# Expert 0's rows picked by fp32 one-hot matmuls from SBUF instead of a gather, and three overflow branches nested in one

## The chip, the cores and the metric

The kernel runs on one core of a Trainium2 chip. The metric is the device time of one execution in microseconds. Three runs of the kernel before took 800.53, 800.73 and 804.94 us, a median of 800.73 us.

## What is computed

One encoder layer on 512 tokens of width 1024 in fp32: a mixer (grouped attention and a spatial gating unit), a cross-attention on 256 memory rows, and a hierarchical mixture of experts, with a last norm. Only the mixture is touched here. `h` below is `rms_norm(x, g_moe)`.

```python
def hierarchical_moe(h, w_rg, b_rg, w_re, b_re, w_gate, w_up, w_down):
    t = h.reshape(B * S, D)
    glog = (t @ w_rg + b_rg).astype(jnp.float32)
    gprob = jax.nn.softmax(glog, axis=-1)
    gval, gidx = lax.top_k(gprob, 1)                       # one of 4 groups
    elog = (t @ w_re + b_re).astype(jnp.float32).reshape(-1, N_GROUPS, EXPERTS_PER_GROUP)
    elog_sel = jnp.take_along_axis(elog, gidx[:, :, None], axis=1)[:, 0]
    evals, eidx = lax.top_k(elog_sel, TOP_K)               # two of its 4 experts
    ew = jax.nn.softmax(evals, axis=-1) * gval
    ...
    for e in range(N_EXPERTS):                             # 16
        he = jax.nn.silu(t @ w_gate[e]) * (t @ w_up[e])
        y = y + combine[:, e:e + 1] * (he @ w_down[e])
```

Each token goes to 2 of 16 experts, so an expert has 64 tokens on average. The kernel gives each expert a block of 128 places.

## The kernel before

**Layout and precision.** The tokens stand in 4 tiles of 128 (`NT`), the width in 8 slices of 128 (`KT`). An fp32 product is made of three fp32r matmuls (`mm3`, L214): high times high, low times high, high times low, where `split` (L210) makes the high part on ScalarE and the low part, the difference, on VectorE. Programs follow the order in which they are written, engine by engine, except that the instructions behind the overflow block form a second sequence.

**Weights.** `Weights` (L68) streams chunks of 1 MB, 128 x 2048, in one fixed order through SP's queue (`issue`, L91) into slots that hold raw chunks, 14 in the expert stage. `pump` (L101) converts half a chunk: ScalarE copies the high part (L113), VectorE subtracts to get the low part (L114; for one half per expert GpSimd does). `hold_low` puts the low parts off until `flush_low`. A finished half gives back its place for converted weights (`done`, L145), of which there are 6, and the next half is converted. `W.limit` bounds how far ahead chunks are fetched. Every expert has chunks 0 and 1 (gate), 2 and 3 (up), 4 and 5 (down).

**Routing.** `wco(t)` (L961) makes the last product of the cross-attention for token tile t, adds it to `xr`, and calls what the caller hangs in between. `rtrans` transposes the tile, `rlog` multiplies it with the router's weights (L996, L997), `rms_scale` (L268) squares the row on ScalarE and makes the norm's scale on VectorE, `h3out` (L984) writes the normed rows to `h3d` in HBM. `route` finds the two experts of each token (L1018 to L1027, 22 small VectorE instructions for two tiles), `route_hi` marks which is the higher, `pos` counts each token's place in its expert's block with triangular matmuls (L1045, L1048).

**From routing to experts.** For expert e, `oh_e` builds a one-hot matrix of tokens against places on VectorE (L1099), `ids_e` multiplies it with the token numbers on TensorE (L1106) and VectorE writes the result as integers (L1107), `gather` fetches the rows from `h3d` with an indirect DMA on GpSimd's queue (L1111), and `xtr` transposes them on TensorE (L276) and splits them. For expert 0 all of that stands ahead of the overflow block; `ids_e` of experts 1 to 4 (`AHEAD` = 5) stands behind it, and only then `xtr` of expert 0 (L1266).

**Overflow.** If an expert has more than 128 tokens, `overflow` (L1167) takes the others in blocks in a loop. Every engine reads the largest count from SBUF and tests it at L1174, three times in a row. No count is that large with these inputs, and nothing of the blocks is in the trace.

**An expert.** `expert_period(e)` (L1320) runs eight halves of gate and up (`gate_up`), in each 6 matmuls of 512 columns for two slices, with hooks after a half (j, i); `mid` is the Silu, `fin` multiplies gate with up on VectorE (L1286), `h_e` transposes the result (L276), `down_scatter` makes the down product and scatters the rows. `h_e` and `down_scatter` of e - 1 run inside the period of e.

## Time and profile before

| what | value |
|---|---|
| median of 3 runs | 800.73 us |
| the profiled execution, its own time | 801.3 us |
| its span, first to last instruction | 799.6 us |
| TensorE busy | 733.2 us, 92% |
| VectorE busy | 612.0 us, 77% |
| ScalarE busy | 463.3 us, 58% |
| GpSimd busy | 197.2 us, 25% |
| mean granted TensorE clock | 0.968 |
| bytes moved by DMA | 161.99 MB, 203 GB/s on average |

All times in rows are microseconds from the start of the span. TensorE's matmuls overlap, so the length of a group in a timeline includes the tail of its last matmul. A clock of 1.00 is 2.4 GHz, 0.50 is 1.2 GHz. The 1.7 us between span and execution lie outside the first and last instruction.

### The profile page before, as it was taken

How to read it: one execution, taken by the hardware profiler on the slowest of the kernel's cores; microseconds unless marked ns; L12 is line 12 of the kernel's file. 1: busy time of each engine (PE TensorE's matmuls, PEld its weight loads, DVE VectorE, ACT ScalarE, POOL GpSimd, SP SyncE). 2: the span in 40 equal slices, each digit the busy share in tenths (PEclk: the TensorE clock that was granted, in tenths of full speed). 3: DMA queues.
4: the chain of work that ended last, by engine and by line, in shares of the span. 5: the costliest groups of instructions: out<-in, count | busy, mean ns of one | idle time of the engine just before them, and what ended most of it. 6: DMA issues, size and time to landing. Idle time of an engine off the chain costs nothing. (4 is left out here: it accounts for less than half of the span.)

```text
span 799.6 us, 10588 instructions
## 1 busy us (share of the span) xinstructions
PE 733.2 (92%) x3839; PEld 610.4 (76%) x3840; DVE 612.0 (77%) x1029; ACT 463.3 (58%) x702; POOL 197.2 (25%) x136
## 2 busy tenths in 40 slices
PE   4887999999999999989999658999999999999891
PEld 4775899778788888889988546888878888888660
DVE  5869899988562434676775758998999999999766
ACT  4545676665433223343554327878878888887742
POOL 4425312231000010032221212333333322222332
PEclk9999999999999999998999869999999999999996
DMA  7303121111212245256237868999889999993082
GB/s 285 129 4 155 54 106 53 55 53 53 95 66 103 106 178 207 88 213 223 71 106 270 310 240 311 334 374 364 334 335 391 356 358 372 389 382 155 14 304 106
DMA packets 28430, 161.99 MB, mean 203 GB/s; under 512 B 5119, under 2 KB 5151, under 8 KB 12112
## 3 DMA queue, kind: packets, MB, share of 16 engines
q1 hardware_dynamic: 21392, 143.66, 47.8%
q0 software_dynamic: 6976, 17.54, 6.0%
q8 instruction: 33, 0.54, 0.3%
q14 instruction: 29, 0.24, 0.1%
HBM read 155.15 MB, written 14.16 MB: 212 GB/s over the span
## 5 line engine op out<-in xcount | busy, mean ns | idle before, releaser
L114 DVE TENSOR_TENSOR l_e<-r_e,h_e 128x1024 fp32r<-128x1024 f32 x178 | 227.7, 1324 | 24.1 <-ACT h_e L113 24.0
L113 ACT ACTIVATE h_e<-r_e 128x1024 fp32r<-128x1024 f32 x192 | 195.5, 1055 | 18.4 <-PE u_e L219 10.4
L1111 POOL DMA_INDIRECT xe<-h3d,ixall x16 | 24.6, 1538 | 137.5 <-PE pt_xt_e L276 94.6
L217 PE MATMUL g_e<-h_e,xh_e 128*128 128x512 f32 x128 | 52.3, 408 | 0.0
L217 PE MATMUL u_e<-h_e,xh_e 128*128 128x512 f32 x128 | 51.6, 403 | 0.0
L218 PE MATMUL g_e<-l_e,xh_e 128*128 128x512 f32 x128 | 50.9, 397 | 0.8 <-DVE l_e L114 0.8
L219 PE MATMUL g_e<-h_e,xl_e 128*128 128x512 f32 x128 | 50.8, 397 | 0.0
L218 PE MATMUL u_e<-l_e,xh_e 128*128 128x512 f32 x128 | 50.6, 395 | 0.0
L219 PE MATMUL u_e<-h_e,xl_e 128*128 128x512 f32 x128 | 50.6, 395 | 0.0
L217 PE MATMUL y_e<-h_e,hh_e 128*128 128x512 f32 x120 | 48.7, 406 | 1.7 <-ACT h_e L113 1.7
L218 PE MATMUL y_e<-l_e,hh_e 128*128 128x512 f32 x120 | 47.5, 396 | 0.8 <-DVE l_e L114 0.8
L114 POOL TENSOR_TENSOR l_e<-r_e,h_e 128x1024 fp32r<-128x1024 f32 x14 | 33.6, 2401 | 57.1 <-ACT h_e L113 57.1
L219 PE MATMUL y_e<-h_e,hl_e 128*128 128x512 f32 x120 | 47.4, 395 | 0.0
L560 ACT ACTIVATE p<-s,nm,qsc 128x512 f32<-128x512 f32 x32 | 25.0, 782 | 35.6 <-DVE nm L557 20.5
L1133 POOL DMA_INDIRECT ybuf<-y,ixall x15 | 31.2, 2083 | 26.0 <-ACT y L1309 23.9
L211 ACT ACTIVATE xh_e<-pt_xt_e 128x512 fp32r<-128x512 f32 x32 | 17.5, 595 | 30.6 <-PE pt_xt_e L276 30.5
L1309 ACT ACTIVATE y<-y_e 128x512 f32<-128x512 f32 x30 | 18.0, 599 | 23.6 <-PE y_e L219 23.6
L218 PEld LDWEIGHTS g_e<-l_e,xh_e 128*128 128x128 f32 x128 | 24.2, 189 | 6.2 <-DVE l_e L114 1.2
L219 PEld LDWEIGHTS g_e<-h_e,xl_e 128*128 128x128 f32 x128 | 24.2, 189 | 6.0 <-DVE xl_e L212 0.2
L219 PEld LDWEIGHTS u_e<-h_e,xl_e 128*128 128x128 f32 x128 | 24.1, 188 | 5.8
L217 PEld LDWEIGHTS g_e<-h_e,xh_e 128*128 128x128 f32 x128 | 24.3, 190 | 5.4 <-ACT xh_e L211 0.4
L218 PEld LDWEIGHTS u_e<-l_e,xh_e 128*128 128x128 f32 x128 | 24.1, 188 | 5.2
(431 smaller groups left out, 2144.3 us busy)
## 6 DMA issues: line engine op xcount, KB each, us to landing
r_e<-in_we_dram SPq DMA_DIRECT2D x95, 1024.0 KB, 8.0
r_a<-in_wf_dram SPq DMA_DIRECT2D x4, 1024.0 KB, 5.5
r_b<-in_wf_dram SPq DMA_DIRECT2D x4, 1024.0 KB, 4.8
r_y<-in_wf_dram SPq DMA_DIRECT2D x4, 1024.0 KB, 4.7
r_wo<-in_wf_dram SPq DMA_DIRECT2D x4, 1024.0 KB, 4.8
yt<-ybuf SPq DMA_DIRECT2D x4, 1024.0 KB, 11.1
xt<-in_x_dram SPq DMA_DIRECT2D x4, 512.0 KB, 5.7
r_q<-in_wf_dram SPq DMA_DIRECT2D x2, 1024.0 KB, 8.1
```

The lines of the kernel that those rows point to most:

```text
L113: A.activation(h, rr, AF.Copy)
L114: lo = lambda X=G if onpool >> i & 1 else V, l=l, rr=rr, h=h: X.tensor_tensor(l, rr, h, op=ALU.subtract)
L211: A.activation(dst_h, src, AF.Copy)
L217: T.matmul(ps, ah, bh, start=first and i == 0, stop=False)
L218: T.matmul(ps, ah, bl, start=False, stop=False)
L219: T.matmul(ps, al, bh, start=False, stop=last and i == n - 1)
L560: A.activation(pr, ps, AF.Exp, bias=nm, scale=qsc[t][:, h:h + 1], accum_out=sx)
L1111: G.indirect_dma_start(out=xe, out_offset=None, in_=h3d, in_offset=bass.IndirectOffsetOnAxis(ap=ix[:, 0:1], axis=0), bounds_check=S - 1, o ...
L1133: return G.indirect_dma_start(out=ybuf, out_offset=bass.IndirectOffsetOnAxis(ap=ix[:, 1:2], axis=0), in_=y, in_offset=None, bounds_check=2 ...
L1309: down(e, lambda n, ps: A.activation(y[:, n * 512:(n + 1) * 512], ps, AF.Copy), pumps)
```

## The change

The rows that `h3out` makes stay in SBUF: they are put into two borrowed raw slots (`borrow`), two token tiles each, until expert 0 has been picked, and still go to `h3d` for the other experts. Expert 0's transposed block is no longer gathered and transposed: `onehot_f32` builds an fp32 one-hot of two token tiles against expert 0's places, and `select(t, g)` multiplies four 128-wide slices of the rows with it into a PSUM bank (`xacc[g]`), summing over the four token tiles. Its two banks are split straight into `xT[0]`. `pos` and the one-hot of tiles 0 and 1 are hung into `wco(3)`; the transposes of tile 3 are copied by ScalarE instead of VectorE; `rlog(3)` uses a part of the bank of `pos`. `flush_low` moves behind the overflow block. Ahead of the experts only `ids_e` of 1 and 2 are left; those of 3 and 0 are hooks of expert 0's period, those of e + 4 of period e, and expert 1's `xtr` moves from hook (1, 1) to (2, 1). Chunks are fetched up to (0, 5) ahead of the experts instead of (2, 2). The two deeper overflow tests are nested in the first.

```diff
--- before.py
+++ after.py
@@ -31,7 +31,7 @@
 POOLJ = 1
 RSQ_MAGIC = float(0x5F3759DF - 2 ** 31)
 FILL_RATE = 1.4
-AHEAD = 5
+AHEAD = 4
 NR3 = 8
 NR4 = 2
 NTH = 6
@@ -82,6 +82,10 @@
         def spare(self, name, shape, dt=F32):
             pl, tag = self.raw_free.pop(0)
             return pl.tile(shape, dt, tag=tag, name=name)
+
+        def borrow(self, name, shape, dt=F32):
+            slot = self.raw_free.pop(0)
+            return slot[0].tile(shape, dt, tag=slot[1], name=name), slot
 
         def take(self, name, shape, dt=F32):
             pl, tag = self.raw_free.pop(0)
@@ -958,7 +962,7 @@
 
     h3T, h3r = {}, {}
 
-    def wco(t, between=None, after=None):
+    def wco(t, hooks):
         for n in range(2):
             w = W.chunk(cid[f"co{n}"])
             ps = bank("SO"[n], f"wc{t}_{n}")
@@ -967,22 +971,21 @@
             V.tensor_tensor(xs, ps, xs, op=ALU.add)
             if t == NT - 1:
                 W.done2(cid[f"co{n}"], 0)
-            if n == 0 and between:
-                between()
-        if after:
-            after()
+            for fn in hooks.get(n, ()):
+                fn()
         h3r[t] = rms_scale(xr[:, t, :], jkb, f"h3{t}")
 
     def rtrans(t):
         for g in range(0, KT, 4):
             pt = tr4(xr[:, t, :], g, f"h3{t}")
-            if t < NT - 1:
-                A.activation(h3T["t"][:, t % 2, g:g + 4], pt, AF.Copy)
-            else:
-                V.tensor_copy(h3T["t"][:, t % 2, g:g + 4], pt)
+            A.activation(h3T["t"][:, t % 2, g:g + 4], pt, AF.Copy)
+
+    h3s = {}
 
     def h3out(t):
-        jk = cr.tile([P, D], F32, tag="P2", bufs=2, name=f"h3{t}")
+        if t % 2 == 0:
+            h3s["t", t // 2], h3s["s", t // 2] = W.borrow(f"h3s{t // 2}", [P, 2, D])
+        jk = h3s[t] = h3s["t", t // 2][:, t % 2]
         if t < NT - 1:
             A.activation(jk, xr[:, t, :], AF.Copy, scale=h3r[t])
             G.tensor_tensor(jk, jk, gmoe, op=ALU.mult)
@@ -990,8 +993,8 @@
             V.scalar_tensor_tensor(jk, xr[:, t, :], h3r[t], gmoe, op0=ALU.mult, op1=ALU.mult)
         nc.sync.dma_start(h3d[t * P:(t + 1) * P, :], jk)
 
-    def rlog(t):
-        pl = bank("F", f"lg{t}")
+    def rlog(t, pl=None):
+        pl = bank("F", f"lg{t}") if pl is None else pl
         for k in range(KT):
             T.matmul(pl[:, :20], h3T["t"][:, t % 2, k], wrs[:, k], start=k == 0, stop=k == KT - 1)
         V.scalar_tensor_tensor(lgt[:, t, :], pl[:, :20], h3r[t], brs, op0=ALU.mult, op1=ALU.add)
@@ -1048,54 +1051,79 @@
         V.scalar_tensor_tensor(posm[:, c], pp[:, ts[0] * NE:(ts[-1] + 1) * NE].rearrange("p (t e) -> p t e", e=NE),
                                1.0, M[:, c], op0=ALU.add, op1=ALU.mult)
 
-    wco(0, lambda: (t2u(3, 0), t2u(3, 1)), lambda: pv2u(1))
+    wco(0, {0: [lambda: (t2u(3, 0), t2u(3, 1))], 1: [lambda: pv2u(1)]})
     cb_s.close()
     raw3 = ctx.enter_context(pool("raw3", side=L))
     W.add_raw(raw3, NR3, "ry")
     h3T["t"] = cr.tile([P, 2, KT, P], F32, tag="h3T", name="h3T")
+
     def upto(key):
         W.limit = cid[key] + 1
         W.issue()
 
-    def out_then(t, *keys):
-        h3out(t)
-        for k in keys:
-            upto(k)
-
-    upto((1, 3))
+    ohf = {}
+
+    def onehot_f32(e, i):
+        ohf[i] = ohp.tile([P, 2, P], F32, tag="oh", name=f"ohf{i}")
+        V.tensor_tensor(ohf[i], io128[:, None, :].to_broadcast([P, 2, P]),
+                        posm[:, 2 * i:2 * i + 2, e:e + 1].to_broadcast([P, 2, P]), op=ALU.is_equal)
+
+    xacc = {}
+
+    def select(t, g):
+        if t == 0:
+            xacc[g] = bank("F", f"xa{g}", (P, 4, P))
+        for k in range(4):
+            T.matmul(xacc[g][:, k, :], h3s[t][:, (4 * g + k) * P:(4 * g + k + 1) * P], ohf[t // 2][:, t % 2],
+                     start=t == 0 and k == 0, stop=t == NT - 1 and k == 3)
+
+    upto((0, 5))
     W.pump(2)
-    wco(1, lambda: (rtrans(0), out_then(0, (0, 5))))
+    wco(1, {0: [lambda: rtrans(0), lambda: h3out(0)]})
     rlog(0)
-    wco(2, lambda: (rtrans(1), out_then(1, (2, 0))))
+    wco(2, {0: [lambda: rtrans(1), lambda: h3out(1)]})
     rlog(1)
+    ohp = ctx.enter_context(pool("ohp", bufs=2, side=L))
     route((0, 1), V)
-    wco(3, lambda: (rtrans(2), out_then(2, (2, 1))), lambda: (rlog(2), rtrans(3)))
+    wco(3, {0: [lambda: rtrans(2), lambda: h3out(2), lambda: pos((0, 1)), lambda: onehot_f32(0, 0)],
+            1: [lambda: rlog(2), lambda: rtrans(3)]})
+    W.hold_low()
     route_hi((0, 1), V)
     V.tensor_tensor(Ms, M[:, 0], M[:, 1], op=ALU.add)
     cd_s.close()
     mx = ctx.enter_context(pool("moex", bufs=2, side=L))
     xes = [mx.tile([P, D], F32, bufs=1, name=f"xe{i}") for i in range(2)]
+    xslot = W.hl_free.pop(0)
+    rlog(3, pp[:, 64:84])
+    h3out(3)
+    W.pump(2)
+    G.memset(xes[1], 0.0)
     G.memset(xes[0], 0.0)
-    h3out(3)
-    G.memset(xes[1], 0.0)
-    xslot = W.hl_free.pop(0)
-    upto((2, 2))
-    W.hold_low()
-    W.pump(2)
-    rlog(3)
+    select(0, 0)
+    select(0, 1)
+    select(1, 0)
     route((2, 3), V)
-    route_hi((2, 3), V)
-    pos((0, 1))
     pos((2, 3))
     for t in (None, 2, 3):
         T.matmul(cnt[:, :NE], ones, M[:, t] if t else Ms, start=not t, stop=t == NT - 1)
+    select(1, 1)
+    onehot_f32(0, 1)
+    cmaxi = rt_([P, 1], "cmaxi", I32)
+    cmax = rt_([P, 1], "cmax")
+    cnts = rt_([P, NE], "cnts", I32)
+    V.tensor_reduce(cmax, cnt[:, :NE], axis=AX.X, op=ALU.max)
+    V.tensor_copy(cmaxi, cmax)
+    route_hi((2, 3), V)
+    for g in range(2):
+        for t in (2, 3):
+            select(t, g)
 
     cr_s.close()
     mo = ctx.enter_context(pool("moe", bufs=2, side=R))
     scat = []
 
     def onehot(name, pos):
-        oh = mx.tile([P, NT, P], F16, tag="oh", name=f"oh_{name}")
+        oh = ohp.tile([P, NT, P], F16, tag="oh", name=f"oh_{name}")
         V.tensor_tensor(oh, io128[:, None, :].to_broadcast([P, NT, P]), pos[:, :, None].to_broadcast([P, NT, P]),
                         op=ALU.is_equal)
         return oh
@@ -1144,17 +1172,8 @@
     def ids_e(e):
         ixs[e] = ids(f"e{e}", ohs[e], lambda t: vals[:, t, e, :], ixall[:, e])
 
-    oh_e(0)
-    cmaxi = rt_([P, 1], "cmaxi", I32)
-    cmax = rt_([P, 1], "cmax")
-    cnts = rt_([P, NE], "cnts", I32)
     posd = dr.tile([NE, P, NT], F32, name="posd")
     vald = dr.tile([NE, P, NT * 2], F16, name="vald")
-    V.tensor_reduce(cmax, cnt[:, :NE], axis=AX.X, op=ALU.max)
-    V.tensor_copy(cmaxi, cmax)
-    ids_e(0)
-    gather(ixs[0], xes[0])
-    W.flush_low()
 
     def overflow_tables(buf):
         pse = buf[:, :NE * NT].rearrange("p (e t) -> p e t", t=NT)
@@ -1170,15 +1189,15 @@
         xt = [mo.tile([P, KT, P], F32R, tag=n, bufs=1, name=f"ov{n}") for n in ("xh", "xl")]
         ht = [mo.tile([P, 4, P], F32R, tag=n, bufs=1, name=f"ov{n}") for n in ("hh", "hl")]
         nover = nc.values_load(cmaxi[0:1, 0:1], min_val=0, max_val=S)
-        for b in range(1, NT):
-            with tc.If(nover > b * P):
-                if b == 1:
-                    overflow_tables(oa)
-                    V.tensor_copy(cnts, cnt[:, :NE])
-                with tc.For_i(0, NE, 1) as ev:
-                    nev = nc.values_load(cnts[0:1, bass.ds(ev, 1)], min_val=0, max_val=S)
-                    with tc.If(nev > b * P):
-                        overflow_block(b, ev, oa, hl, xt, ht)
+        with tc.If(nover > P):
+            overflow_tables(oa)
+            V.tensor_copy(cnts, cnt[:, :NE])
+            for b in range(1, NT):
+                with tc.If(nover > b * P):
+                    with tc.For_i(0, NE, 1) as ev:
+                        nev = nc.values_load(cnts[0:1, bass.ds(ev, 1)], min_val=0, max_val=S)
+                        with tc.If(nev > b * P):
+                            overflow_block(b, ev, oa, hl, xt, ht)
 
     def overflow_block(b, ev, oa, hl, xt, ht):
         pe = sm.tile([P, NT], F32, tag="pe", name=f"pe{b}")
@@ -1209,7 +1228,7 @@
         split(ht[0], ht[1], tr4(g, 0, f"h_o{b}"))
         y = xo
         for n in range(2):
-            ps = bank("F", f"y{n}_o{b}")
+            ps = bank("T", f"y{n}_o{b}")
             for i, w in oc(4 + n):
                 proj(ps, ht, 2 * i, w, i == 0, i == 1)
             A.activation(y[:, n * 512:(n + 1) * 512], ps, AF.Copy)
@@ -1221,14 +1240,19 @@
     manual.enter_context(tc.manual_schedule())
     W.add_raw(raw4, NR4, "rz")
     W.limit = len(W.order) - 1
+    xh0, xl0 = (mo.tile([P, KT, P], F32R, tag=f"x{n}", bufs=1, name=f"x{n}_e0") for n in "hl")
+    for g in range(2):
+        split(xh0[:, 4 * g:4 * g + 4], xl0[:, 4 * g:4 * g + 4], xacc[g])
+    xT[0] = xh0, xl0
+    W.flush_low()
+    W.raw_free += [h3s["s", i] for i in range(2)]
     W.issue()
     oh_e(1)
     ids_e(1)
     gather(ixs[1], xes[1])
     W.pump(1)
-    for e in range(2, AHEAD):
-        oh_e(e)
-        ids_e(e)
+    oh_e(2)
+    ids_e(2)
     d = rt_([P, NT], "d")
     eg = rt_([P, NT, 4], "eg")
     gval = rt_([P, NT], "gval")
@@ -1263,7 +1287,6 @@
         V.tensor_tensor(tq, w2, lt, op=ALU.mult)
         V.tensor_tensor(whi, whi, tq, op=ALU.add)
 
-    xT[0] = xtr("e0", xes[0])
     W.pump(1)
 
     def gate_up(e, js, hooks):
@@ -1323,13 +1346,17 @@
             W.nhold = 1
         hooks = {(0, 0): [], (2, 0): [lambda: mid(e)]}
         if e == 0:
+            hooks[1, 0] = [lambda: oh_e(3)]
+            hooks[1, 1] = [lambda: ids_e(3), lambda: oh_e(0)]
+            hooks[3, 0] = [lambda: ids_e(0)]
+        if e == 0:
             gather(ixs[2], xes[0])
         if e + AHEAD < NE:
             hooks[0, 0] = [lambda: oh_e(e + AHEAD)]
             hooks[2, 1] = [lambda: ids_e(e + AHEAD)]
         hooks[0, 1] = [lambda: h_e(e - 1) if e else combine_exps()]
         if e == 0:
-            hooks[1, 1] = [lambda: xT.update({1: xtr("e1", xes[1], xslot)})]
+            hooks[2, 1] += [lambda: xT.update({1: xtr("e1", xes[1], xslot)})]
         if e == 5:
             hooks[3, 1] = [combine_weights]
         if e == NE - 2:
```

## Rows read from the trace of the kernel before

**Rows 1.** Busy time by 20 us: engine busy us (instructions), TensorE clock, DMA share, GB/s.
```profile
460.00:480.00 20.00, 11.68 (x64) 9.46 (x65) 11.76 (x19) 5.68 (x9) 3.55 (x3) 0.69 0.66 246
...
500.00:520.00 20.00, 20.00 (x96) 16.10 (x96) 18.95 (x21) 17.09 (x22) 6.64 (x4) 1.00 0.91 333
```

**Rows 2.** Waits of the SP queue, 500 to 725: total us, times, longest.
```profile
SPq L97 <- DVE l_e L114: 193.3, 72, 9.9
```

**Rows 3.** Timeline of TensorE, 443 to 509: start, us, line, operation, count, idle before and releaser.
```profile
443.65 1.04 PE L276 MATMUL pt_h<-identf,xr 128*128 128x128 f32 x8
...
449.02 1.07 PE L276 MATMUL pt_h<-identf,xr 128*128 128x128 f32 x8
...
450.44 2.16 PE L996 MATMUL lg<-wrs,h3T 128*128 128x20 f32 x16 [0.35 <-DVE h3T L982]
...
469.12 0.27 PE L1106 MATMUL ids_e<-vals,oh_e 128*128 128x2 f16 x4 [0.85 <-DVE oh_e L1099]
...
469.24 1.95 PE L276 MATMUL pt_xt_e<-identf,xe 128*128 128x128 f32 x8
...
471.15 0.79 PE L217 MATMUL g_e<-h_e,xh_e 128*128 128x512 f32 x1
...
477.47 1.04 PE L276 MATMUL pt_xt_e<-identf,xe 128*128 128x128 f32 x8
...
489.99 0.66 PE L276 MATMUL pt_h_e<-identf,g 128*128 128x128 f32 x4 [2.15 <-DVE g L1286]
...
508.22 0.60 PE L276 MATMUL pt_h_e<-identf,g 128*128 128x128 f32 x4
```

**Rows 4.** Timeline of POOL, 460 to 466: the gathers of experts 0 and 1.
```profile
460.49 1.32 POOL L1111 DMA_INDIRECT xe<-h3d,ixall  x1 [9.86 <-ACTq L1174]
...
465.87 1.24 POOL L1111 DMA_INDIRECT xe<-h3d,ixall  x1 [4.06 <-DMA xe<-h3d,ixall]
```

**Rows 5.** Timeline of VectorE, 444 to 480, columns as in the timeline of TensorE.
```profile
444.98 0.37 DVE L1027 SCALAR_TENSOR_TENSOR M<-io,i,ro 128x16 bf16<-128x16 f32 x2
...
450.89 0.14 DVE L262 TENSOR_SCALAR v_h<-ss_h 128x1 f32<-128x1 f32 x1
...
454.47 0.27 DVE L1018 TENSOR_REDUCE gm<-lgt 128x1 f32<-128x4 f32 x2
...
456.59 0.37 DVE L1027 SCALAR_TENSOR_TENSOR M<-io,i,ro 128x16 bf16<-128x16 f32 x2
...
458.14 0.19 DVE L1048 SCALAR_TENSOR_TENSOR posm<-pos,M 128x32 f32<-128x32 f32 x1 [0.37 <-PE pos L1045]
...
459.57 2.36 DVE L114 TENSOR_TENSOR l_e<-r_e,h_e 128x1024 fp32r<-128x1024 f32 x2
...
463.87 0.69 DVE L1099 TENSOR_TENSOR oh_e<-io,posm 128x512 f16<-128x512 bf16 x1 [1.95 <-DVEq L1174]
...
467.26 0.68 DVE L1099 TENSOR_TENSOR oh_e<-io,posm 128x512 f16<-128x512 bf16 x1
...
471.13 1.42 DVE L212 TENSOR_TENSOR xl_e<-pt_xt_e,xh_e 128x512 fp32r<-128x512 f32 x2 [1.55 <-ACT xh_e L211]
...
478.93 2.36 DVE L114 TENSOR_TENSOR l_e<-r_e,h_e 128x1024 fp32r<-128x1024 f32 x2 [1.25 <-ACT h_e L113]
```

**Rows 6.** Timeline of ScalarE, 444 to 449: copies of the transposes, the row's squares.
```profile
444.29 1.09 ACT L980 ACTIVATE h3T<-pt_h 128x512 f32<-128x512 f32 x2 [3.08 <-PE pt_h L276]
...
448.48 1.04 ACT L270 ACTIVATE jkb<-xr 128x1024 bf16<-128x1024 f32 x1
```

**Rows 7.** Timeline of TensorE, 170 to 200: the fp32 matmuls of 128 columns.
```profile
175.30 1.05 PE L536 MATMUL vm<-bw,vg 128*128 128x128 f32 x8
```

**Rows 8.** Busy time by half microseconds: TensorE clock falling and rising again.
```profile
452.00:452.50 0.50, 0.50 (x7) 0.50 (x7) 0.46 (x3) 0.00 (x0) 0.00 (x0) 0.55 0.98 344
...
472.50:473.00 0.50, 0.50 (x3) 0.38 (x3) 0.05 (x1) 0.00 (x0) 0.00 (x0) 0.97 0.94 393
```

**Rows 9.** Instructions of line 1174, the branches: queue, kind, count, ns min/median/max, first and last start.
```profile
L1174 DVEq COMPARE_BRANCH  x3: 56/56/72, 460.4 to 462.6; - x3
```

## The prediction

> **What bounds the kernel now.** I read the busy times by stretches first, because the chain of waits covers only the end of this kernel. In the expert stage TensorE is busy 20.00 of 20 us [rows 1], and the SP queue spends 193 of 225 us waiting for VectorE to free a raw slot [rows 2]: weights lie ready, TensorE is the bound, and whatever delays or hastens its first gate matmul moves the end. The stretch before it is another matter: TensorE is busy 11.68 of 20 us there, at a mean clock of 0.69 [rows 1].
>
> So I read the timelines of that stretch. The router's last matmuls run from 450.44 to 452.6; the first gate matmul of expert 0 starts at 471.15 [rows 3]. Who ends that gap? The gather of expert 0 is issued at 460.49, and the next gather, which waited for its landing, starts at 465.87 [rows 4]. But the transposes of the gathered rows start only at 469.24, directly behind `ids_e` of expert 4 at 469.12 [rows 3]. TensorE stood in its own order behind the ids of experts 1 to 4, and these go at VectorE's pace: one-hot, ids, integers, from 463.87 on, one round in a little over 1.1 us [rows 5]. The gather was in by 465.87; it was not the last wait. VectorE is: route, one-hot, 2.36 us of low parts, branches, one-hots [rows 5]. That is what the change has to shorten.
>
> **The change part by part**, on the time axis of the trace before.
>
> *Ahead of route.* `pos((0,1))` now stands on TensorE behind `rtrans(2)`, which is through at about 444.45 (443.65 and 8 transposes, the tail left out) [rows 3]. It needs `M`, ready at 444.98 + 0.37 = 445.35 [rows 5]. `wco(3)`'s second half, `rlog(2)` and `rtrans(3)` queue behind it: with three tiny matmuls 1.0 us late. `rtrans(3)` goes from 449.02 [rows 3] to 450.0. Its two copies on ScalarE (0.55 each by 1.09 for two) end at about 451.65, and the square of tile 3, 1.04 us, now stands behind them instead of at 448.48 [rows 6]. The norm's chain on VectorE starts at 452.8 instead of 450.89 [rows 5]: 1.9 us late. VectorE's two copies are gone, but they lay in the shade of that square. The rest up to the end of `route` is the same instructions in another order, so `M` of tiles 2 and 3 comes at 456.96 + 1.9 = 458.9.
>
> *Counting.* From `M` to `posm` it took 458.33 - 456.96 = 1.4 us, with `route_hi` and the first `posm` in between [rows 5]. Both now stand elsewhere; 0.4 remains: 459.3 instead of 458.33. The second fp32 one-hot (half of the 0.69 of a 128 x 512 one) is done at 459.7, while `select(1,1)` runs.
>
> *Selecting.* A select is 4 fp32 matmuls of 128 columns, 8 instructions; 8 such took 1.05 us with the tail [rows 7], so 0.9 apart. The three that stand ahead of `route` have room from 453 to 458.9, at half clock too (5.4 us). Five stand behind `M`: 4.5 us at full clock, 9.0 at half. The clock had fallen by 452.5 [rows 8], while the router's 20-column matmuls ran; the selects are 128 columns wide and begin at just that point, so I take the full clock: done at 463.6. Half is the other bound: 468.1.
>
> *Splitting.* The first bank is split under the last selects. The second costs 0.55 on ScalarE and 1.42 / 2 = 0.71 on VectorE [rows 5, 6]: 464.9. The transposes of expert 0, the gather and the ids of expert 0 are off TensorE's way; that is the gain.
>
> *What is late next.* `flush_low` comes behind the splits in VectorE's order, then the one-hots and ids of experts 1 and 2, and TensorE meets both ids before the first gate half. Low parts: 2.36 us. From the one-hot of expert 1 to that of expert 3 it took 467.26 - 463.87 = 3.39 us, one low part included; TensorE is released 0.2 earlier, so 3.2 [rows 5]. First gate matmul: 464.9 + 2.36 + 3.2 = 470.5, against 471.15: a gain of 0.65 us. Most of what the gather's path gave up is taken by a chain that was there before and now starts later.
>
> *The branches.* Between the end of the low parts at 461.93 and the one-hot at 463.87 VectorE spent 1.9 us on three tests [rows 5, 9]. One remains, and the other two cost nothing because every engine's test lies in the shade of the selects: VectorE's at about 460.8, TensorE's at 463.6 with 4 us until its next ids. Without that cover a test would cost at most those 1.9 us.
>
> *The clock at the start.* Before, TensorE's work resumed at 469.24 and the clock was back at 472.5 [rows 3, 8]; of that 1.35 us lay behind 471.15, a loss of 0.7. After, TensorE idles from 463.6, and its first work but for ids is the gate matmul itself: 3.26 us at half clock, a loss of 1.6, so 0.9 more. If the selects keep it up, 0.7 less than before.
> The Trainium skill (TensorE: Matmul & The Clock Gate, Part 4: PE-mode transpose) says that transposes do not count as busy for the clock. By that rule the 8 transposes before did nothing for the clock, 1.35 us of gate matmuls raised it, the loss stays 0.7 and the sum is 0.9 lower. The trace fits both: the clock rose 1.35 us behind the first gate matmul and 3.26 us behind the first transpose.
>
> *Inside expert 0.* Two one-hots and two ids move in from the front. `ids_e(3)` stands at hook (1, 1), which TensorE reached at 477.47, where before it had the transposes of expert 1; its one-hot stands on VectorE behind the low part that began at 478.93 [rows 3, 5]. With 1.2 and 0.6 us it is ready at about 480.7: a stall of 3.2. Before, TensorE stood 2.15 us ahead of `pt_h` at 489.99 [rows 3], waiting for VectorE; a stall in hook (1, 1) lets conversions catch up, so these largely replace each other. Bounds: 0 and 3.2; I take 1.5, nearer to the old stall given back than to both paid. Expert 1's transposes, moved to (2, 1), come some 13 us behind the first gate matmul; its gather is issued near 468.5 and the first one needed 5.4 us from issue [rows 4], so it is hidden.
>
> *At nothing.* GpSimd loses one gather and waits anyway. Three chunks less are fetched ahead, but ten lie ready, some 30 us of work at 3 us each (an expert's period of six chunks is 18.2 us, from `pt_h` at 489.99 to the next at 508.22 [rows 3]), while the first late one is asked for at about 461 to 467. The borrowed slots come back before they are needed. The blocks of the overflow do not run. One ids less and `AHEAD` leave the later periods as they are.
>
> *Sum.* -0.65 + 0.9 + 1.5 = +1.75 us. On the profiled execution's 801.3 that is 803.05; the median lies 0.6 below it, so 802.5. With every bound on one side: -0.65 - 0.7 + 0 = -1.35, and -0.65 + 4.5 + 0.9 + 3.2 = +7.95.
>
> **Rivals.** *The selects release the experts (faster).* If VectorE did the low parts and the one-hots of experts 1 and 2 while the selects run, the first gate half would follow the splits at 464.9, on a warm clock: -6.25 - 0.7 + 1.5 = -5.45, 795.3. For it speaks VectorE's idleness from 460.8 to the first split; against it the order in which they are written. It decides from the point where the ids of experts 1 and 2 are out before 464.9.
> *Half clock under the selects (slower).* The clock fell here before at 452, and it stays down if the gap between the third and the fourth select counts as idle. Five selects then end at 468.1: +1.75 + 4.5, 807.0. Against it: the gap is no longer than about 3 us.
> *Weights late (slower).* DMA is 0.91 busy in the first periods [rows 1], and three chunks have to be made up. If the lead is used up, three chunks cost their own 9.5 us (3 x 1.05 MB at 333 GB/s [rows 1]) on top of the sum: 812. It decides when a chunk lands more than 25 us after its issue; the wait for slots [rows 2] speaks against it.
>
> **How the numbers follow.** The forecast has 0.65, the faster rival 0.13, half clock 0.13, late weights 0.06, the rest 0.03. About 1% (8 us) is what a measurement of this kernel can tell from no change. Faster by over 1% needs the faster rival and expert 0's stall gone as well: 0.07. Slower by over 1% is late weights and the far end of half clock: 0.10. Within 1%: 0.83. The range, 796 to 808, takes the bounds of the sum and half clock, and leaves out late weights and most of the faster rival.
>
> **What would show it.** In the changed kernel's timelines: `M` of tiles 2 and 3 near 458.9; the last select near 463.6, or 468 at half clock; then TensorE idle until the ids of expert 2, released by VectorE's one-hots and not by a DMA; the first gate matmul near 470.5; a stall of some 3 us at `ids_e(3)` and a short one ahead of `pt_h`; TensorE full from then on. I am wrong if the first gate matmul comes before 466 or behind 474, or if ScalarE or VectorE wait for a chunk's DMA among the first three experts.

## The result and the profile after

The changed kernel takes 809.95 us (median), the kernel before 802.75 us: ratio 1.0091, interval 1.0066 to 1.0116. One of the changed kernel's six runs took 1877.74 us; the ratio leaves it out, and without it the median is 809.56. The kernel is slower by some 7 us, just inside the 1% called no change, and 2 us above the range. The profiled execution's span is 808.5 us against 799.6.

The busy times of the changed kernel by 20 us, columns as in [rows 1]:

```profile
460.00:480.00 20.00, 10.50 (x59) 8.84 (x58) 8.72 (x16) 3.89 (x5) 2.33 (x2) 0.74 0.44 173
480.00:500.00 20.00, 16.44 (x80) 12.44 (x79) 14.05 (x20) 12.73 (x17) 4.20 (x2) 0.91 0.87 342
500.00:520.00 20.00, 20.00 (x98) 16.21 (x97) 18.38 (x19) 17.46 (x22) 5.21 (x3) 1.00 0.91 326
```

From 500 us on TensorE is full, as in [rows 1]. The time went in the 40 us before. The first window has 10.50 us of work against 11.68 [rows 1], although the end of the selects stands in it; the second has 16.44, at a mean clock of 0.91. In the kernel before it was

```profile
480.00:500.00 20.00, 17.20 (x87) 13.61 (x86) 17.52 (x19) 15.74 (x18) 4.23 (x2) 1.00 0.86 312
```

The timeline of TensorE in the changed kernel, to be read against [rows 3]:

```profile
453.78 5.17 PE L1077 MATMUL xa<-ohf,h3s 128*128 128x128 f32 x24
...
458.99 4.72 PE L1077 MATMUL xa<-ohf,h3s 128*128 128x128 f32 x40
471.04 0.27 PE L1134 MATMUL ids_e<-vals,oh_e 128*128 128x2 f16 x4 [7.33 <-DVE oh_e L1127]
473.31 0.27 PE L1134 MATMUL ids_e<-vals,oh_e 128*128 128x2 f16 x4 [2.01 <-DVE oh_e L1127]
473.74 0.77 PE L221 MATMUL g_e<-h_e,xh_e 128*128 128x512 f32 x1 [0.16 <-issue]
474.30 0.63 PE L222 MATMUL g_e<-l_e,xh_e 128*128 128x512 f32 x1
...
478.99 0.39 PE L221 MATMUL g_e<-h_e,xh_e 128*128 128x512 f32 x1
...
484.80 0.25 PE L1134 MATMUL ids_e<-vals,oh_e 128*128 128x2 f16 x4 [2.85 <-DVE oh_e L1127]
...
486.04 0.63 PE L222 MATMUL u_e<-l_e,xh_e 128*128 128x512 f32 x1
...
497.12 0.66 PE L280 MATMUL pt_h_e<-identf,g 128*128 128x128 f32 x4 [0.28 <-DVE g L1309]
```

The last select ends at 463.71, the first gate matmul starts ten us later, its successors cost 0.63 us (half clock, 0.427 us apart) until 478.99 instead of 0.39 (0.233 apart), and a second such stretch follows the stall at 484.80. `pt_h` comes at 497.12 against 489.99 [rows 3]: 7.1 of the 7.2 us are lost by then. What released the split that stands between select and gate? The timelines of ScalarE and VectorE:

```profile
466.19 1.09 ACT L215 ACTIVATE xh_e<-xa 128x512 fp32r<-128x512 f32 x2 [11.87 <-PEq L1192]
```
```profile
460.54 0.20 DVE L1038 TENSOR_TENSOR vals<-vals,ro 128x32 f16<-128x32 f16 x1
466.82 1.29 DVE L216 TENSOR_TENSOR xl_e<-xa,xh_e 128x512 fp32r<-128x512 f32 x2 [6.09 <-ACT xh_e L215]
468.03 2.35 DVE L118 TENSOR_TENSOR l_e<-r_e,h_e 128x1024 fp32r<-128x1024 f32 x2
470.29 0.69 DVE L1127 TENSOR_TENSOR oh_e<-io,posm 128x512 f16<-128x512 bf16 x1
```

Not a select but L1192, the overflow test, on TensorE's queue ("PEq"). That line's instructions (count: shortest, median, longest ns; first and last start):

```profile
L1192 ACTq EVENT_SEMAPHORE  x2: 17/17/17, 463.1 to 463.2; - x2
L1192 DVEq EVENT_SEMAPHORE  x2: 21/21/21, 464.3 to 464.4; - x2
L1192 PEldq EVENT_SEMAPHORE  x2: 51/51/51, 466.0 to 466.1; - x2
L1192 DVEq COMPARE_BRANCH  x1: 72/72/72, 461.3 to 461.3; - x1
L1192 PEldq COMPARE_BRANCH  x1: 3632/3632/3632, 462.3 to 462.3; - x1
```

TensorE's test runs from 462.3 to 465.9, and only the events behind it tell ScalarE that TensorE is past the block. VectorE stood idle from 460.74 to 466.82, and its 5.7 us of work (low parts, one-hots and index sums of experts 1 and 2, with the 1.23 us low part between) came only behind the split, from 468.03 on.

### The profile page after: what moved, and what is told of

Same layout as the page of the kernel before. It is cut to its first block, busy times and chain, and to the rows that moved or that the text cites. A ratio compares the mean times of both kernels' runs of the same rounds, so it can differ in the third digit from the quotient of the medians.

```text
span 808.5 us, 10653 instructions
## 1 busy us (share of the span) xinstructions
PE 745.2 (92%) x3895; PEld 621.0 (77%) x3896; DVE 610.9 (76%) x1029; ACT 464.6 (57%) x704; POOL 190.0 (23%) x135
## 5 line engine op out<-in xcount | busy, mean ns | idle before, releaser
L1161 POOL DMA_INDIRECT ybuf<-y,ixall x15 | 25.5, 1701 | 27.5 <-ACT y L1332 25.4
L221 PEld LDWEIGHTS u_e<-h_e,xh_e 128*128 128x128 f32 x128 | 24.3, 190 | 5.2
```

The lines of the kernel that those rows point to most:

```text
L221: T.matmul(ps, ah, bh, start=first and i == 0, stop=False)
L1161: return G.indirect_dma_start(out=ybuf, out_offset=bass.IndirectOffsetOnAxis(ap=ix[:, 1:2], axis=0), in_=y, in_offset=None, bounds_check=2 ...
```

## The experiments

The theories: **1**, the tests stand between selects and split, and the split waits for TensorE's; **2**, VectorE's chain stands behind the split although VectorE was idle before; **3**, TensorE runs at half clock after standing still, at the start and after the stall at `ids_e(3)`. Rivals: the nested form costs; weights are late; the gather, not the chain, was the last wait in the kernel before. In the table, times count from the start of `wco(3)`'s second add on VectorE, the last work that all kernels share (447.51 in the kernel before, 448.07 in the changed one); they are differences of rows of each timeline. The kernel before ran beside each group and took 802.75 to 803.81 us. The three columns of times come from one profiled execution of each kernel, and that one can lie off the median: it took 808.99 us for busy gap and 805.72 for "the same, more rounds".

| kernel | split starts | first gate matmul | `pt_h` | median us | ratio to before, interval |
|---|---|---|---|---|---|
| before | | 23.6 | 42.5 | 802.75 | |
| changed | 18.1 | 25.7 | 49.1 | 809.95 | 1.0091 (1.0066 to 1.0116) |
| no overflow | 13.7 | 22.3 | 45.2 | 803.89 | 1.0015 (1.0000 to 1.0031) |
| flat tests | 21.0 | 28.5 | 51.9 | 812.33 | 1.0120 (1.0096 to 1.0144) |
| split first | 15.6 | 23.7 | 47.0 | 807.53 | 1.0063 (1.0035 to 1.0091) |
| late ids | 17.5 | 25.2 | 45.2 | 805.47 | 1.0033 (1.0016 to 1.0049) |
| busy gap | 17.6 | 28.9 | 49.7 | 812.37 | 1.0129 (1.0108 to 1.0149) |
| chain first | 17.5 | 18.4 | 41.0 | 802.08 | 0.9987 (0.9974 to 1.0000) |
| before, late ids | | 21.5 | 42.8 | 802.68 | 0.9990 (0.9978 to 1.0003) |
| before, nested | | 23.8 | 43.7 | 804.57 | 1.0026 (1.0014 to 1.0038) |
| all three | 13.9 | 18.4 | 37.9 | 798.74 | 0.9940 (0.9917 to 0.9963) |
| all three b | 13.6 | 17.8 | 35.3 | 798.22 | 0.9970 (0.9928 to 1.0011) |
| the same, more rounds | 16.1 | 21.9 | 40.6 | 799.97 | 0.9944 (0.9931 to 0.9958) |
| chain and ids | 21.5 | 22.2 | 40.9 | 802.04 | 0.9991 (0.9978 to 1.0004) |

**No overflow block.**

```diff
-    manual.close()
-    overflow()
-    manual.enter_context(tc.manual_schedule())
```

> The changed kernel with the overflow block left out altogether: tokens of an expert beyond its first 128 are not worked on, so no engine has a test or a jump between the selects and the split. Theory 1 (the split waits for TensorE's jump): in the changed kernel the last select ends at 463.7 and ScalarE's split starts at 466.2, released by TensorE's queue at the jump; without it the split starts at about 463.9, VectorE's chain behind it (two low parts, two weight low parts, one-hot, ids) moves up by the same 2.3 us, the first gate matmul comes at about 471.4 in place of 473.7, and the run is 2 to 3 us shorter, about 807.4. The prediction's own view (the tests lie in the shade of the selects): the first gate matmul stays within 0.5 us of 473.7 and the time within 1 us of the changed kernel's 810.0.

ScalarE's splits in its timeline:

```profile
460.92 0.60 ACT L215 ACTIVATE xh_e<-xa 128x512 fp32r<-128x512 f32 x1 [7.47 <-PE xa L1077]
462.58 0.60 ACT L215 ACTIVATE xh_e<-xa 128x512 fp32r<-128x512 f32 x1 [1.06 <-PE xa L1077]
```

Theory 1 holds: the splits now wait for selects, the first gate matmul comes 3.4 us sooner, `pt_h` 3.9. The run is 6 us shorter, twice the forecast. Its profiled execution is 7.5 us shorter than the changed kernel's: 0.9 ahead of the add, 3.9 from there to `pt_h`, 0.4 in the experts that follow and 2.4 behind the `pt_h` of expert 14, where TensorE stayed at full clock.

**Flat tests.** Nested form against three in a row, all else as changed (the code is that of the kernel before).

> The changed kernel with the three overflow tests one after another again, as before the change, and all else as it is. Rival theory N (nesting is what costs: one jump over a larger body takes longer than three short ones): the 3.6 us of TensorE's queue at the one jump fall to the three tests' 3.1 us of the kernel before, and the split starts 0.5 us sooner; if nesting alone were the cause of the 2.4 us wait, the split would start at 463.9 and the run would be 2 to 3 us shorter. Theory 1 (it is the place of the tests between the selects and the split that costs, whatever their form): the last far jump stays, the split starts within 0.7 us of 466.2 and the time stays within 1.5 us of 810.0, in either direction.

TensorE's tests in this kernel, and the split:

```profile
L1193 PEldq EVENT_SEMAPHORE  x6: 51/51/51, 463.0 to 468.5; - x6
L1193 PEldq COMPARE_BRANCH  x3: 353/1877/2783, 461.5 to 465.5; - x3
```
```profile
468.56 1.08 ACT L215 ACTIVATE xh_e<-xa 128x512 fp32r<-128x512 f32 x2 [14.72 <-PEq L1193]
```

Slower by 2.4 us, beyond the 1.5 allowed, in the direction against the rival: nesting does not cost here, it saves. The three tests run from 461.5 to 468.3; the first takes 0.35 us, but its events start at 463.0, as the selects end (462.93), so the others stand behind the selects.

**Before, nested.** The same edit in the kernel before.

> The kernel before the change with the overflow tests nested in one, and nothing else changed. With the changed kernel in both forms it completes a table of two by two (place of the tests, form of the tests). The prediction's view (the form changes nothing): the one-hot behind VectorE's tests stays within 1 us of its place and the time within 1 us of before. Rival from the runs so far (the nested form saved 2.4 us in the changed kernel): there the second and third test stood behind the selects on TensorE's queue and the split waited for them; in the kernel before nothing waits for TensorE's test, and VectorE's one-hot waited 1.9 us for VectorE's, so the nested form can save at most about 1 us, or lose 1 us since VectorE's one jump takes 2.9 us in the changed kernel.

VectorE's first one-hot behind the block:

```profile
464.30 0.69 DVE L1099 TENSOR_TENSOR oh_e<-io,posm 128x512 f16<-128x512 bf16 x1 [2.11 <-PEq L1173]
```

TensorE's one test takes 3.8 us there, and the one-hot, which waits for it now, starts 0.2 us later (16.5 against 16.4 behind the add). The time is 1.1 to 3.1 us above before by its interval. Without the selects the form gains nothing; of the 1.2 us by which `pt_h` is later, 1.0 come inside expert 0, where more of its matmuls ran at half clock. That nesting pays only where other work holds the second and third test back fits both pairs, and was not tested further.

**Split first.** `xslot` goes to expert 0, so that the split needs none of the block's tiles.

```diff
+    xh0, xl0 = (xslot[0].tile([P, KT, P], F32R, tag=n + xslot[1], name=f"x{n}_e0") for n in "hl")
+    for g in range(2):
+        split(xh0[:, 4 * g:4 * g + 4], xl0[:, 4 * g:4 * g + 4], xacc[g])
+    xT[0] = xh0, xl0
     raw4 = ctx.enter_context(pool("raw4", side=L))
     manual.close()
     overflow()
...
-        split(xh0[:, 4 * g:4 * g + 4], xl0[:, 4 * g:4 * g + 4], xacc[g])
...
```

> The changed kernel with expert 0's split (two ScalarE roundings, two VectorE low parts) issued ahead of the overflow block instead of behind it; its result goes to the block of chip memory that expert 1 had, and expert 1's to the other. Theory 1 on the split: it starts at about 463.9 in place of 466.2. But VectorE's own test, which now runs in VectorE's idle time (461.3 to 464.3), comes to stand behind the low parts, at about 466, and ends near 469; the weights' low parts then start at about 469 in place of 468.0, and the first gate matmul comes at 474 to 475, the time 0 to 2 us longer than the changed kernel's 810.0. Rival (the split alone holds the gate matmuls): the first gate matmul comes 2.3 us sooner, at 471.4, and the time is about 807.5.

```profile
463.78 0.60 ACT L215 ACTIVATE xh_e<-xa 128x512 fp32r<-128x512 f32 x1 [9.36 <-PE xa L1077]
467.64 0.60 ACT L215 ACTIVATE xh_e<-xa 128x512 fp32r<-128x512 f32 x1 [3.26 <-ACTq L1192]
```

The numbers are the rival's (first gate matmul 471.88, 807.53 us), and the expectation's were missed, but the edit did not do what either speaks of, so the run is inconclusive. Only the first half came ahead of the test; the second still waited 3.26 us for ScalarE's. And the order of other work shifted: the two low parts moved ahead of the route, which brought `M` 2 us later. The first gate matmul gained 2.0 us all the same, and the time 2.4.

**Late ids.** Inside expert 0: `oh_e(3)` at hook (0, 0), `ids_e(3)` still at (1, 1).

```diff
-            hooks[1, 0] = [lambda: oh_e(3)]
-            hooks[1, 1] = [lambda: ids_e(3), lambda: oh_e(0)]
+            hooks[1, 1] = [lambda: ids_e(3), lambda: oh_e(4)]
...
-            hooks[0, 0] = [lambda: oh_e(e + AHEAD)]
-            hooks[2, 1] = [lambda: ids_e(e + AHEAD)]
+            hooks[0, 0] = [lambda: oh_e(e + AHEAD if e else 3)]
+            hooks[2, 1] = [lambda: ids_e(e + AHEAD)] + [lambda: oh_e(0)] * (not e)
```

> The changed kernel with the one-hots and index sums of experts 3, 4 and the second round's expert 0 spread differently over expert 0's stages, so that no index matmul stands behind a one-hot of the same stage: the one-hot of expert 3 goes out two stages ahead of its index sum. Theory 3 (the 2.85 us stall at expert 3's index matmul, and the half clock that follows it from 485.9 to 489.2, are part of the loss): the stall and the half clock behind it go, the transposes of the activation come at about 492.6 to 494.3 in place of 497.1, and the time is 2.9 to 4.5 us shorter, 805.5 to 807. Rival (weights are late: one ScalarE rounding already waited 1.05 us for its transfer at 494): the stall only moves to the weights and the time stays within 1.5 us of 810.0.

```profile
481.18 0.25 PE L1134 MATMUL ids_e<-vals,oh_e 128*128 128x2 f16 x4
...
485.40 0.25 PE L1134 MATMUL ids_e<-vals,oh_e 128*128 128x2 f16 x4 [1.07 <-DVE oh_e L1127]
```

As theory 3 expected: `ids_e(3)`, at 481.18, waits for nothing, no half clock follows, `pt_h` comes at 493.28, 3.9 us sooner by the table, and the run is 4.5 us shorter. A stall of 1.07 us is left, at `ids_e(4)`. Late weights would not have let this through.

**Busy gap.**

> The changed kernel with 48 extra fp32 matmuls of 128x128 (the identity on itself, into a bank that nothing reads) in TensorE's gap between the selects and expert 0's first gate matmul: 36 behind the overflow block, 12 between the index sums of experts 1 and 2. At full clock they take 0.118 us each, 4.2 and 1.4 us, and fit into the gap (466.0 to 471.0 and 471.3 to 473.3). Theory 3 (TensorE runs at half clock from the first gate matmul at 473.7 to 479.0 because it stood still before): with the gap filled the first twelve gate matmuls of 512 columns take 0.23 us each in place of 0.43, 2.3 us less, and the time is about 807.6. The second half-clock stretch behind expert 3's index sum stays as it is. Rival (the half clock has nothing to do with the gap, or the extra matmuls, at half clock, push the gate matmuls later): the first gate matmuls stay at 0.43 us and the time at 810 to 813.

TensorE's timeline, the extra work being `warm`:

```profile
465.37 8.28 PE L1252 MATMUL warm<-identf 128*128 128x128 f32 x72 [2.50 <-PEq L1192]
473.49 0.24 PE L1134 MATMUL ids_e<-vals,oh_e 128*128 128x2 f16 x4
473.59 2.92 PE L1256 MATMUL warm<-identf 128*128 128x128 f32 x24
476.35 0.24 PE L1134 MATMUL ids_e<-vals,oh_e 128*128 128x2 f16 x4
476.45 0.47 PE L221 MATMUL g_e<-h_e,xh_e 128*128 128x512 f32 x1
476.77 0.39 PE L222 MATMUL g_e<-l_e,xh_e 128*128 128x512 f32 x1
...
485.48 0.25 PE L1134 MATMUL ids_e<-vals,oh_e 128*128 128x2 f16 x4 [3.19 <-DVE oh_e L1127]
485.59 0.48 PE L221 MATMUL u_e<-h_e,xh_e 128*128 128x512 f32 x1
485.90 0.40 PE L222 MATMUL u_e<-l_e,xh_e 128*128 128x512 f32 x1
```

I had taken one instruction for one matmul; an fp32 matmul is two, 0.23 us, so the filling took 10.9 us in place of 5.6 and the time got worse. But it tells what it was made for: at the end of a busy gap the gate matmuls run at full clock (0.39 and not 0.63 us), so it is the idle gap that the half clock followed. The kernels below in which the gap is short, 2.5 us in chain first and 2.4 to 3.7 in all three, begin at full clock too. `pt_h` is only 0.7 us late though the first gate matmul is 3.2 late. These 2.6 us are not the price of the first stretch alone: the second stretch, which was expected to stay, is gone too, some 3.8 us for both, and the stalls in expert 0 are 1.1 us longer in sum. And the stall at `ids_e(3)`, 3.19 us here, is followed by full clock: a stall of that size need not bring the clock down.

**Chain first.**

```diff
...
+    W.flush_low()
+    oh_e(1)
+    oh_e(2)
     raw4 = ctx.enter_context(pool("raw4", side=L))
     manual.close()
     overflow()
...
-    W.flush_low()
...
-    oh_e(1)
...
-    oh_e(2)
```

> The changed kernel with VectorE's chain brought ahead of the overflow block: the two held weight low parts (2.35 us) and the one-hots of experts 1 and 2 are issued before the tests, in the 6 us in which VectorE stood idle (460.7 to 466.8); the overflow block makes its own one-hot in a buffer of its own so that it doesn't take theirs. Theory 2 (of the 10 us from the last select to the first gate matmul some 5.5 are VectorE's chain behind the split, and VectorE had the time for it before): the low parts are done at 463.2, VectorE's test ends at about 467.3 in place of 464.3, its low parts of the split at 468.6, expert 2's one-hot at 469.7, the first gate matmul comes at about 470 in place of 473.7, and the time is 3 to 5 us shorter, 805 to 807. Rival (VectorE's test now comes late and takes the place of the chain): the first gate matmul stays within 1 us of 473.7.

VectorE and TensorE:

```profile
459.30 2.35 DVE L118 TENSOR_TENSOR l_e<-r_e,h_e 128x1024 fp32r<-128x1024 f32 x2
461.56 0.69 DVE L1127 TENSOR_TENSOR oh_e<-io,posm 128x512 f16<-128x512 bf16 x1
463.20 0.69 DVE L1127 TENSOR_TENSOR oh_e<-io,posm 128x512 f16<-128x512 bf16 x1 [0.95 <-DVEq L1192]
```
```profile
464.82 0.37 PE L1134 MATMUL ids_e<-vals,oh_e 128*128 128x2 f16 x8 [2.46 <-PEq L1192]
465.40 0.47 PE L221 MATMUL g_e<-h_e,xh_e 128*128 128x512 f32 x1 [0.21 <-ACT xh_e L215]
```

Theory 2, by twice its forecast: the first gate matmul comes 7.3 us sooner, not 3.7. VectorE's test did not take the chain's place. It held VectorE for 0.95 us only, because part of its jump passed while the low parts were still running, and both one-hots were out before TensorE's own test ended. The run is 8 us shorter than the changed one, and level with the kernel before.

**Before, late ids.** `oh_e`, `ids_e` of experts 3 and 4 moved into expert 0's hooks.

> The kernel before the change, with the one-hots and index sums of experts 3 and 4 moved from ahead of expert 0's transposes into its stages. It tells which of two waits stood last ahead of expert 0 in the kernel before. The prediction's view (VectorE's one-hots paced it, not the gather, rows 3 and 5): the transposes of expert 0's tokens start 2.2 us sooner, at 467.0, the first gate matmul at 468.9, and the time falls by up to 2.2 us, to about 801. Rival (the gather is the last wait): the transposes wait for the gathered rows instead and the time stays within 0.7 us of before.

```profile
467.07 0.27 PE L1106 MATMUL ids_e<-vals,oh_e 128*128 128x2 f16 x4 [1.99 <-DVE oh_e L1099]
467.19 1.95 PE L276 MATMUL pt_xt_e<-identf,xe 128*128 128x128 f32 x8
...
487.49 0.25 PE L1106 MATMUL ids_e<-vals,oh_e 128*128 128x2 f16 x4 [3.00 <-DVE oh_e L1099]
```

The transposes follow the index sums 2.2 us sooner: the chain was the last wait there, not the gather. The time does not fall: expert 0 gives the gain back, by 1.2 us more of stalls, 3.00 at the moved index sum, and by half clock behind the first gate matmul, 3.5 us of it against 1.4.

**All three.** Split and chain first, `ids_e(2)` and its gather behind the first stage, the others as in late ids and spread further; then the version that also moves `ids_e(4)` to hook (3, 1) and expert 0's pair into expert 1's stages, and that with the split behind the block again.

> The changed kernel with all the causes taken together: expert 0's split and VectorE's chain (two weight low parts, one-hot of expert 1) issued ahead of the overflow block, expert 2's index sum and gather moved from ahead of the first gate matmul to behind the first stage, experts 3, 4 and 0's spread over the stages of experts 0 and 1. If theories 1 to 3 hold together: first gate matmul at about 468 in place of 473.7, no 2.85 us stall at expert 3's index sum and no half clock behind it, so the transposes of the activation at about 487.5 to 489 in place of 497.1 (490.0 in the kernel before), and the time 799 to 801, faster than the kernel before by 0.2 to 0.6 %. Rival (the weights, or VectorE's test, then set the pace): the time stays at 803 to 806, no better than the best single part.

> The version with all parts taken together, with its one remaining stall in expert 0 taken away: there expert 4's index sum still waited 1.35 us for its one-hot, which VectorE reached late; it now goes one stage later, and expert 0's second pair into expert 1's stages. If the stalls of index sums inside expert 0 are what the rest of the loss is: transposes of the activation another 1.3 to 2 us sooner than in the version before (37.9 us behind the last add of the third cross-attention stage), at 36 to 36.6, and the time 796.5 to 797.5. If the weights set the pace by then: unchanged, 798.7 within 0.7.

> The same as the run beside it, but with expert 0's split back behind the overflow block, where the change put it. If VectorE's chain is what mattered ahead of the first gate matmul (it came 18.4 us behind the last add both with the split ahead and with it behind): the first gate matmul and the time stay within 0.7 us of the run beside it. If the place of the split is worth its wait of 2 us for TensorE's jump: 1.5 to 2.5 us slower.

> The version with all parts and the later index sum once more, in more rounds, since its interval (0.9928 to 1.0011) still held no change. If what its trace showed holds (the activation's transposes 7.2 us sooner than in the kernel before, 35.3 against 42.5 us behind the last add, and no half clock among expert 0's gate matmuls), the time is 797.5 to 799.5 and the ratio 0.993 to 0.996, and the clock is full again from the first gate matmul on. If the full clock there was an accident of that execution, the first gate matmuls run at 0.63 us for a few us and the time is 1 to 1.5 us longer.

The first is faster than the kernel before by 0.4 to 0.8%, the second by 0.4 to 0.7% in the longer comparison: 799.97 against 803.81 us. Both kernels of this case are beaten, the changed one by some 10 us. The second gains 2.6 us over the first at `pt_h`, but 0.5 in the medians: in its trace expert 0's index sum, now among expert 1's stages, waits there for its one-hot,

```profile
488.06 0.25 PE L1134 MATMUL ids_e<-vals,oh_e 128*128 128x2 f16 x4 [1.69 <-DVE oh_e L1127]
```

and from `pt_h` to that of expert 14 it takes 256.25 us, the first 254.44. Its two profiled executions differ. In one, of 798.22 us, the selects took 4.71 us, TensorE's test 3.4 and the gate matmuls ran at full clock; in the other, of 805.72 us,

```profile
458.87 7.46 PE L1077 MATMUL xa<-ohf,h3s 128*128 128x128 f32 x40
470.06 0.24 PE L1134 MATMUL ids_e<-vals,oh_e 128*128 128x2 f16 x4 [3.73 <-PEq L1192]
...
471.71 0.63 PE L221 MATMUL g_e<-h_e,xh_e 128*128 128x512 f32 x1
```

the selects ran largely at half clock, the test took 5.2 us, and half clock came back under the gate matmuls: the accident that the last expectation allowed for. With the split behind the block (chain and ids) the test took 6.2 us, and the median is 3.8 us above its neighbour's, where "worth its wait" had 1.5 to 2.5. The neighbour's interval (0.9928 to 1.0011) is too wide to tell these apart; against its longer comparison the difference is 0.5% (0.9991 and 0.9944). How much of it is the longer test and how much the place of the split, one profile each can't say.

## Why the prediction was wrong, point by point

The sum said 1.75 us more, and 7.2 were measured. The 2 us by which the time lies above the range are no more than the kernel before moved by: its median went from 800.73 to 802.75 us with three more runs. And 7.2 us are less than the sum's far bound of 7.95, but only by luck: 4.5 of that bound are half clock under the selects, which did not come, and nothing in it stands for the wait of the split.

**Right up to the last select.** `M` ended at 458.54 (predicted 458.9), the one-hot followed, the last select ended at 463.71 (463.6), five selects at full clock. That three selects ran at half clock (5.17 us for 24 instructions) cost nothing, as room had been left. The rival of half clock under the five was not what happened in the changed kernel's profile, but two later kernels show it (6.3 and 7.5 us): one of the two kernels (all three b) had full clock there in another execution, so it is a matter of the execution.

**The branches are the first step that failed.** "Cost nothing" was argued from who *executes* a test: TensorE's had cover until its next index sum. But the split on ScalarE reads TensorE's banks, and behind the block it waits for the events that TensorE sends when it is past the block. The bound of 1.9 us came from VectorE's tests alone [rows 9]. The split started at 466.19 and not behind the last select at 463.7: 2.5 us; and its first half, which was to lie under the selects, stood behind the test too: 0.7 more. The low parts of the split were done at 468.1 instead of 464.9. No overflow shows it.

**The chain had the right size** (5.6 us from the splits to the gate, predicted and measured) and began 3.2 us late with the split. First gate matmul: 473.74 for 470.5, just short of the 474 that was to be the sign of being wrong. The prediction saw that VectorE was idle and named the version with the chain ahead as its faster rival; chain first shows that this is what the written order gave away, 7.3 us.

**The clock at the start was mis-sized.** Predicted 3.26 us at half clock, measured 5.25 (473.74 to 478.99): a loss of 2.3 us instead of 1.6. Both figures come from one execution each. Behind the first gate matmul of the kernel before half clock lasted 1.4 us, 3.5 in its variant with late ids and 4.7 in the nested one; of the changed kernel 5.3, and 3.5 to 6.0 in no overflow, flat tests, split first, late ids and chain and ids. So how much of the difference is the change's stays open.
The prediction weighed a rule of the Trainium skill (TensorE: Matmul & The Clock Gate, Part 4: PE-mode transpose), that transposes do not count as busy in the same way. By it, gate matmuls alone raised the clock in 1.35 us before, and should have again, without transposes ahead. The runs do not decide on it: 1.4, 3.5 and 4.7 us were measured behind the same 8 transposes.

**Inside expert 0 a term was missing.** The stall at `ids_e(3)` came as predicted (2.85 for 3.2) and the old one at `pt_h` went (0.28 for 2.15). What was not in the sum is that half clock can follow a stall of this size: seven matmuls of 512 columns from 486.04 on, and two in part, lose up to 0.194 us each, 1.5 us in all. Late ids removes both. Half clock also followed this stall in no overflow, flat tests, split first and chain first (2.59 to 3.00 us), but not in busy gap (3.19) and not the 3.00 us in before, late ids. From first gate matmul to `pt_h` expert 0 took 23.4 us against 18.8: 4.5 more, of which the start's clock is 1.6, the second stretch 1.5, the stalls 0.8 and two more index sums 0.3; 0.3 I can't place.

**The sum, made again:** 0.6 at the add, 2.0 from there to the first gate matmul, 4.5 in expert 0, 7.1 at `pt_h`; the medians differ by 7.2. The rival of late weights did not come: ScalarE waited once for a transfer, 1.05 us at 494.15, which the prediction had named as a sign of being wrong, and TensorE not at all. The profiled execution's further 1.6 us, behind the `pt_h` of expert 14 at 751.21, are not the change's: after a 1.68 us stall at 753.49, which the kernel before has too, seven matmuls ran at half clock, and so did seven or eight in both variants of the kernel before that ran here, though none in its own profile.

## What to carry to other kernels

A test that is never taken still splits the program: ask not only which engine executes it and under what cover, but which consumer behind it reads what an engine ahead of it wrote; that consumer waits until the producer's engine is past the block. Put work that is ready ahead of such a block, above all on the engine that idles there. And price every stall of some 3 us on TensorE with the half clock that may follow it, here another 1.5 us behind the stall and 2.3 behind the gap.

## What the hardware showed that I had not expected

TensorE's jump over the unused block is long: 3.4 to 3.8 us in most kernels here with the nested form, 5.2 and 6.2 in two. It is 3.8 in before, nested, too, where no selects stand ahead of it. In the changed kernel the test's own record on the other engines is 50 to 72 ns, and on ScalarE, VectorE and SP 2.4 to 3.0 us pass until their next event. The DMA queues of the changed kernel from 458 to 470 show what goes on (packets, MB, share):

```profile
q14 instruction: 7, 0.06, 1.4%
q8 instruction: 2, 0.03, 1.0%
```

In the kernel without the block there is no instruction transfer in that stretch, so these come with the block.
The Trainium skill (Runtime: NRT & Kernel Launch, Instruction fetch mechanics) says that a taken branch to a target outside the prefetched code makes the engine wait for a DMA fetch of it. The trace fits that, 9 transfers of 0.09 MB in all, but shows no wait that ends with one of them.
What lengthened TensorE's test to 5.2 and 6.2 us stays open. In both executions weights streamed at up to 437 GB/s meanwhile, but so they did in chain first, where it took 3.4. Both are also those whose last five selects ran in part at half clock (7.46 and 6.34 us against 4.7 elsewhere); whether one brings the other is not shown.
